# ifftshift of an 8192 x 8192 matrix by DMA alone: half rows in 512 KB DMAs with SBUF copies between them

## The chip, the cores and the metric

The kernel runs on one core of a Trainium2 chip. The metric is the device time in microseconds of one execution, lower is better. A profile of one execution comes with the times.

## The reference

```python
def setup_inputs():
    return {"x": np.random.randn(8192, 8192).astype(np.float32)}

def reference(x):
    return np.fft.ifftshift(x)
```

Both axes have an even length, so the four quadrants change places: output row r, left half, is input row (r + 4096) mod 8192, right half; and the right half comes from the left half of the same input row. Nothing is computed. 268.4 MB are read and as many written.

## The kernel before

The kernel is a set of DMAs from the input in HBM to the output in HBM; nothing passes through SBUF and no compute engine takes part. The unit is a half row: 4096 floats, 16 KB, contiguous in input and output.

One DMA (`copy`, issued on L29) moves 256 half rows, 4 MB. Its pattern is `[[C, 16], [16*C, 16], [1, 4096]]`: the outermost dimension has 16 entries, one for each of the core's 16 DMA engines, and engine e moves rows e, e+16, e+32, ... of the block, 16 half rows in all.

The loop on L36 to L39 goes through the rows in parts of 1024, four DMAs for each queue. SP's queue (`nc.sync`) moves left output halves, in row order. ACT's queue (`nc.scalar`) moves right output halves, and takes the four blocks of a part in the order 2, 3, 0, 1, so that it is 512 rows away from SP.

The two queues are independent of each other: each engine has one ring of descriptors for each of them. The order within a queue is the order of the program. The scheduler gives each queue four completion semaphores, so at most four DMAs of a queue are in flight; the issue of the next waits until the oldest has landed on all 16 engines.

Of the kernel before, what the change touches and what calls it, by code (L numbers as in the profile page):

```python
# [1 line left out]

# [4 lines left out]


ENGINES = 16


@with_exitstack
def kernel(
    ctx: ExitStack,
    tc: tile.TileContext,
    x: bass.AP,
    out: bass.AP,
):
    nc = tc.nc
    R, C = x.shape  # L20
    hr = R // 2
    hc = C // 2
    per = 16
    rows = ENGINES * per

    def copy(queue, row, h, step):

        dims = [[C, ENGINES], [step * C, per], [1, hc]]
        queue.dma_start(  # L29
            out=bass.AP(out.tensor, out.offset + row * C + h, dims),  # L30
            in_=bass.AP(x.tensor, x.offset + (row + hr) % R * C + hc - h, dims),
        )

    for first in range(0, R, 4 * rows):  # L36
        for n in range(4):
            copy(nc.sync, first + n * rows, 0, ENGINES)
            copy(nc.scalar, first + (n + 2) % 4 * rows, hc, ENGINES)  # L39


# [1 line left out]
_INS = ['x']  # L43
_OUTS = [((8192, 8192), 'float32')]


def kernel(**inputs):
    import numpy as _np
    import concourse.bacc as _bacc
    import concourse.tile as _tile  # L50
    from concourse import mybir as _mybir
    from concourse.bass_utils import run_bass_kernel_spmd as _run

    nc = _bacc.Bacc("TRN2", target_bir_lowering=False, num_devices=1)  # L54
    arrays, args = {}, []
    for name in _INS:
        a = _np.ascontiguousarray(inputs[name])
        if a.dtype.kind in "iu":
            a = a.astype(_np.int64)
        arrays[f"in_{name}_dram"] = a  # L60
        args.append(nc.dram_tensor(f"in_{name}_dram", a.shape, _mybir.dt.from_np(a.dtype), kind="ExternalInput").ap())
    for i, (shape, dtype) in enumerate(_OUTS):
        dt = _mybir.dt.from_np(_np.dtype(dtype))
        args.append(nc.dram_tensor(f"out_{i}_dram", shape, dt, kind="ExternalOutput").ap())
    with _tile.TileContext(nc) as tc:
        kernel(tc, *args)
    r = _run(nc, [arrays], core_ids=[0])
    got = tuple(r.results[0][f"out_{i}_dram"] for i in range(len(_OUTS)))
    return got[0]
```

## Time and profile before

| | |
|---|---|
| median of 2 runs | 822.9 us (822.66 and 823.14) |
| span of the profiled execution | 812.4 us |
| time around the span, if the profiled execution took the median | 10.5 us |
| DMAs | 32 on SP's queue, 32 on ACT's, 4 MB each |
| median from issue to landing | 101.0 us on each queue |
| packets | 17,408, 268.44 MB |
| DMA-issuing instruction, median | 571 ns on SP, 578 ns on ACT |

The span runs from the first to the last instruction. "Share of 16 engines" in the DMA part of the page is the time that a queue's packets took, divided by 16 times the span. A packet here is one half row or one semaphore write of 4 bytes. GB/s on the page count each byte once, though it is read from HBM and written to HBM.

### The profile page before, as it was taken

The page shows a single profiled execution, that of the slowest core. Times are in us where ns is not written, and L with a number is a line of the kernel's source. Part 1 is how long each engine was busy: PE and PEld are TensorE (multiplying, and loading weights), DVE is VectorE, ACT ScalarE, POOL GpSimd, SP SyncE. Part 2 cuts the span into 40 slices and gives each one's busy share as a digit, 9 for nine tenths or more (in the row PEclk, how much of TensorE's full clock was granted, in tenths as well). Part 3 has the DMA queues.
Part 4 walks back from the last instruction along what each step waited for, and adds up shares of the span by engine and source line. Part 5 has one row for each costly group of instructions (what it writes and reads, how often), then busy time and mean ns, then how long its engine had stood idle before and what let it go on. Part 6 is the DMA issues. An engine that isn't in the chain of part 4 may idle for free. (4 is left out here: it accounts for less than half of the span.)

```text
span 812.4 us, 109 instructions
## 1 busy us (share of the span) xinstructions
POOL 0.2 (0%) x4
## 2 busy tenths in 40 slices
POOL 0000000000000000000000000000000000000000
DMA  9999999999999999999999999999999999999998
GB/s 307 331 331 336 335 331 331 335 325 337 334 332 336 331 333 332 334 339 332 332 334 331 329 331 334 332 328 333 330 334 335 334 328 333 332 331 330 338 331 280
DMA packets 17408, 268.44 MB, mean 330 GB/s; under 512 B 1024, under 2 KB 1024, under 8 KB 1024
## 3 DMA queue, kind: packets, MB, share of 16 engines
q1 hardware_dynamic: 8704, 134.22, 49.7%
q10 hardware_dynamic: 8704, 134.22, 49.5%
HBM read 268.44 MB, written 268.44 MB: 661 GB/s over the span
## 5 line engine op out<-in xcount | busy, mean ns | idle before, releaser
L54 POOL MEMSET const-bfloat16-1.0<- 128x1 bf16 x1 | 0.1, 101 | 0.0
L54 POOL MEMSET const-uint8-127<- 128x1 uint8 x1 | 0.1, 101 | 0.0
L54 POOL MEMSET const-float32-0.0<- 128x1 f32 x1 | 0.1, 98 | 0.2 <-issue 0.2
L54 POOL MEMSET const-float32-1.0<- 128x1 f32 x1 | 0.1, 98 | 0.0
## 6 DMA issues: line engine op xcount, KB each, us to landing
out_dram<-in_x_dram SPq DMA_DIRECT2D x32, 4096.0 KB, 101.0
out_dram<-in_x_dram ACTq DMA_DIRECT2D x32, 4096.0 KB, 101.0
```

What stands on the lines that cost most here:

```text
L54: nc = _bacc.Bacc("TRN2", target_bir_lowering=False, num_devices=1)
```

## The change

Three things change.

- A DMA moves 32 half rows (512 KB, 2 per engine) instead of 256. The pattern is otherwise the same, and so is the order in which each engine moves its half rows. ACT's queue is still 512 rows from SP's within a part of 1024 rows.
- A tile `idle` of 128 x 2560 floats in SBUF is set to zero by VectorE at the start (L35).
- In the second to the seventh eighth of the rows, each half-row DMA is followed in its queue by a DMA from 16 partitions of `idle` to the same partitions of another SBUF tile (`space`, L49): one piece per engine, of 512, 1024, 1536, 1792, 2048 and 2560 floats, that is 2, 4, 6, 7, 8 and 10 KB. The first and the last eighth have none. The destination tiles come from a pool with six buffers for each of the two queues. What they hold is not used.

The issue order of a step is: SP half rows, ACT half rows, SP copy, ACT copy. Of the four DMAs of a queue in flight, two are then half-row DMAs and two are copies.

```diff
-    per = 16
+    f32 = mybir.dt.float32
+    per = 2
     rows = ENGINES * per
+    longest = 2560
+    still = ctx.enter_context(tc.tile_pool(name="still", bufs=1))
+    spaced = ctx.enter_context(tc.tile_pool(name="spaced", bufs=6))
+    idle = still.tile([128, longest], f32)
+    nc.vector.memset(idle[:], 0.0)
 
-    def copy(queue, row, h, step):
-
-        dims = [[C, ENGINES], [step * C, per], [1, hc]]
+    def copy(queue, row, h):
+        dims = [[C, ENGINES], [ENGINES * C, per], [1, hc]]
+        dst = out.offset + row * C + h
+        src = x.offset + (row + hr) % R * C + hc - h
         queue.dma_start(
-            out=bass.AP(out.tensor, out.offset + row * C + h, dims),
-            in_=bass.AP(x.tensor, x.offset + (row + hr) % R * C + hc - h, dims),
+            out=bass.AP(out.tensor, dst, dims),
+            in_=bass.AP(x.tensor, src, dims),
         )
 
+    def space(queue, n, name):
 
+        into = spaced.tile([128, longest], f32, name=name)
+        queue.dma_start(out=into[0:128:8, :n], in_=idle[0:128:8, :n])
 
-    for first in range(0, R, 4 * rows):
-        for n in range(4):
-            copy(nc.sync, first + n * rows, 0, ENGINES)
-            copy(nc.scalar, first + (n + 2) % 4 * rows, hc, ENGINES)
+    part = 1024
+    for first, n in zip(range(0, R, part), (0, 512, 1024, 1536, 1792, 2048, 2560, 0)):
+        for row in range(first, first + part, rows):
+            other = first + (row - first + part // 2) % part
+            copy(nc.sync, row, 0)
+            copy(nc.scalar, other, hc)
+            if n:
+                space(nc.sync, n, "sync_piece")
+                space(nc.scalar, n, "scalar_piece")
```

## The prediction

> **What bounds the kernel now.** I read the page first (slices, DMA queues, issues), then the waits of the SP queue, then a table of stretches of the span, and last the records of single packets in the trace. No engine computes, so the slices and the queues say it all:
>
> ```profile
> span 812.4 us, 109 instructions
> ...
> DMA  9999999999999999999999999999999999999998
> GB/s 307 331 331 336 335 331 331 335 325 337 334 332 336 331 333 332 334 339 332 332 334 331 329 331 334 332 328 333 330 334 335 334 328 333 332 331 330 338 331 280
> ...
> q1 hardware_dynamic: 8704, 134.22, 49.7%
> q10 hardware_dynamic: 8704, 134.22, 49.5%
> HBM read 268.44 MB, written 268.44 MB: 661 GB/s over the span
> ```
>
> The 16 DMA engines are busy for 99.2% of the span from end to end, half of it for each queue. A half row (4096 floats, 16,384 bytes) is one packet: 16,384 of them, and 1,024 packets of 4 bytes that carry the semaphores (64 DMAs x 16 engines). So one engine moves 1,024 half rows in 0.992 x 812.4 = 806 us, 787 ns each. The packet records give the spread behind that mean: the shortest take 608 to 611 ns, 32% lie within 615 ns, the longest takes 2,064 ns, the standard deviation is 194 ns. So an engine can move a half row in 611 ns (26.8 bytes per ns), and 787 - 611 = 176 ns per half row, 180 us of the 806, is time in which the shared path to memory holds it back. On one engine the half rows of the two queues alternate (96% of neighbours are of different queues), and a 4-byte packet takes 9 ns with no gap before or behind it.
>
> ```profile
> core 0: us, POOL busy (x), PEclk, DMA share, GB/s
> ...
> 3.00:5.00 2.00, 0.00 (x0) 1.00 1.00 393
> 5.00:10.00 5.00, 0.00 (x0) 1.00 1.02 360
> 10.00:20.00 10.00, 0.00 (x0) 1.00 0.99 328
> ```
>
> The stretch from 3 to 5 us has packets of SP's queue alone, 16 engines busy, and shows 393 GB/s; with both queues it falls to 360 and then stays near 330. That is short, and packets are counted where they start, but it says that 330 need not be a wall.
>
> ```profile
> SPq L29 <- DMA out_dram<-in_x_dram: 689.4, 28, 25.3
> ```
>
> Of SP's 32 issues 28 wait: each queue has four DMAs in flight, and the fifth waits for the first to land on its slowest engine.
>
> **The change, part by part.** (1) The main transfers. Row order on every engine, packet size and bytes stay as they are (engine e still moves rows e, e+16, ... of one half, and ACT is still 512 rows from SP). DMAs of 2 instead of 16 half rows per engine make 512 instead of 64. (2) Copies inside SBUF: 64 in each of six eighths, 384 in all, one piece of 2, 4, 6, 7, 8 or 10 KB per engine. They add work to the engines, none to HBM.
>
> *Packets.* Semaphore packets per engine: 512 + 384 = 896 instead of 64, so 832 x 9 ns = 7.5 us more. Copies: 64 x (2+4+6+7+8+10) KB = 2,368 KB per engine. Before shows no copy within SBUF. Its lower price is the engine's fastest rate, 26.8 bytes per ns: 90.5 us. As the upper one I take a copy that is held back as the mean half row is, 16,384/787 = 20.8 bytes per ns: 116.6 us. I take the lower, as a copy does not use the memory path that holds the others back. New engine time: 98 us (124 at the upper price) on 806.
>
> *What of it is given back.* While an engine copies, it does not ask for HBM, and the other 15 queue less. Two bounds: nothing given back, 98 us; all of it given back up to the engine's own floor. For the second, an eighth needs 806/8 = 100.8 us of memory; an engine's own need in the 10 KB eighth is 128 x 0.611 + 64 x 10,240/26.8 ns + 1.2 = 103.8 us, and every other eighth stays below 100.8 (8 KB: 98.9). That bound costs 3 us. In between I use a closed queue: 16 customers (the engines), each 611 ns plus its share of copy away from the crowd, and one shared server of S ns per half row with random service. Waiting for n customers follows from n-1: R = S(1 + Q), X = n/(R + Z), Q = XR, with Z = 611 - S + copy and semaphore time per half row. It gives 787 ns at n = 16 for S = 45.8 ns (358 GB/s each way). The random service is a choice, borne out by the spread: the excess over 611 has a mean of 176 and a deviation of 194 ns, about as an exponential wait has. With the copies in Z, the eighths cost 100.9, 103.7, 106.6, 109.7, 111.4, 113.1, 116.7 and 100.9 us: 863 instead of 806, so +57.5 us. At the upper copy price it is +76 us.
>
> *Issues and the wait.* An issue holds SP 571 ns and ACT 578 (the source line's durations). A pair of main DMA and copy is 1.15 us of issuing per queue, against 2 x 524,288 bytes / 330 GB/s = 3.2 us of moving, so it hides. It would set the pace only if a pair moved in under 1.15 us. The copies stand in the same queues, so four in flight are now two main and two copies. From the last engine's semaphore packet to the next issue of that queue takes 0.8 us (36.68 to 37.48 us in the records), from an issue to its first packet 1.4 us (11.86 to 13.29): 2.2 us. When main DMA i has landed, the slowest engine still has one main DMA and two copies in that queue and as much in the other: four half rows, 3.1 us, plus copies. So the slowest does not run dry; an engine ahead of it by more than 0.9 us may (DMAs land over 1.2 to 2.7 us from first engine to last). A fast engine that pauses is not the one that sets the end, and it eases HBM too; 0 to 10 us, I take 0. The Trainium skill's DMA: Bandwidth & Descriptors, under Rules for kernel authors, wants at least 1 MiB per DMA for the best rate, which speaks against 512 KB; here the packets follow each other over the end of a DMA with no gap, so a row outweighs that rule, and by its fit of 2.0 us plus bytes/436e3 a main DMA alone would be an estimated 3.2 us, just what a queue has for it.
>
> *Hidden at nothing.* The memset of the 128 x 2560 tile lies at the start; the first copy comes after the first eighth, some 100 us later. If it were late, SP and ACT would stop at their first copy with main transfers behind them, and three main DMAs per queue would cover about 10 us. A copy tile is written again after six copies of that name, two more than are in flight. The last eighth has no copies, so the drain of the queues stays as it is.
>
> *Sum.* The profiled execution spans 812.4 us and the median is 822.9, so 10.5 us lie around the span; I leave these alone. 822.9 + 57.5 = 880.
>
> **Rivals.** (A) Hidden: memory moves 661 GB/s whatever the engines do, and the copies fill time in which they would only queue. Then it is +3 to +10 us, 826 to 833. For it: the slices stay within 325 to 339 GB/s. Against: a third of the half rows runs at the engine's own pace, which a path that is always full would not allow. The Trainium skill's HBM Reference, under Specifications (TRN2), gives about 716 GB/s for a domain; the trace's 661 is 92% of it, which leans to this rival.
>
> (B) Nothing given back: the 176 ns are collisions of address patterns, not of numbers of engines. 822.9 + 98 = 921. For it: the mean of a half row changes with its place in the DMA, about 755 to 815 ns by turns. Against: it needs 14 engines in HBM to queue like 16.
>
> (C) Faster, the other side: the spacing takes the two queues out of each other's way, as in the 3 to 5 us stretch. At 393 GB/s a half row takes 16 x 16,384/393 = 667 ns: 1,024 x 0.667 + 98 = 781 against 806, so 798 us. It decides where half rows fall below (806 - 98)/1,024 = 691 ns; over 2% faster needs 675. Against: the fall from 360 to 328 came within 20 us, with both queues in order.
>
> (D) Copies at half rate, because pairs of engines meet in SBUF: 13.4 bytes per ns, 181 us of engine time, by the same queue +126: 949 us. No row of before bears on it. The Trainium skill's SBUF page (SBUF — State Buffer, under Door 1: The DMA port swizzle) has partitions 0, 8, 16, ... on 8 of 16 ports, two engines to each; that would give this rate where both copy at once, and no run here shows it.
>
> **How the numbers follow.** Chances: forecast (840 to 905) 0.43, A 0.20, B 0.13, C 0.17, D 0.07. The range goes from C's 798 to a little over B's 921, 926; it leaves out half of C and most of D, about 0.15. The likeliest case alone, with copy prices of both ends and a third of the give-back either way, is 850 to 905. About 2% is what a measurement of this kernel can tell from no change (806.4 to 839.4): faster 0.17, same 0.20, slower 0.63.
>
> **What would show it.** In the slices the rate should be near 331 GB/s in the first and last eighth and fall step by step between, to about 287 of main bytes in the 10 KB eighth, with the DMA share still 9 throughout. The mean main packet should come down from 787 to about 735 ns, the shortest stay at 611; a 10 KB copy should take about 382 ns. Wrong would be: main packets at 787 (B) or under 691 (C), copies of 760 ns (D), eighths of equal length (A), or DMA shares under 9, where the window of four runs dry.

## The result and the profile after

The changed kernel takes 913.6 us (two runs, 908.0 and 919.3) against 822.9: ratio 1.110, 95% interval 1.094 to 1.126. It is slower, by 91 us. The profiled execution is the one of 919.3 us, with a span of 917.3. So about 2 us lie around a span, not 10.5; the profile of before (812.4 us) was simply one of its quicker executions. The spans of before listed in later runs go from 817.5 to 823.5 us. The changed kernel varies far more: its six executions, these two and the four of the run `again`, take 880.6 to 919.3 us, all at a granted clock of 1.0, so its loss is 58 to 96 us from one execution to the next.

The first view is the page of the changed kernel: span, slices, queues, HBM bytes, and the DMA issues with their size and the median time from issue to landing.

```profile
span 917.3 us, 944 instructions
...
DMA  9999999999999999999999999998999999999998
GB/s 304 324 329 329 334 332 342 350 339 352 347 332 360 339 378 382 320 376 317 307 395 349 302 306 309 337 311 303 351 347 345 330 331 367 313 355 322 327 327 282
...
q10 hardware_dynamic: 18432, 153.65, 50.4%
q1 hardware_dynamic: 18432, 153.65, 46.3%
...
HBM read 268.44 MB, written 268.44 MB: 585 GB/s over the span
...
out_dram<-in_x_dram SPq DMA_DIRECT2D x256, 512.0 KB, 7.9
out_dram<-in_x_dram ACTq DMA_DIRECT2D x256, 512.0 KB, 7.9
```

The slices still show 9 nearly everywhere, but the two queues sum to 96.7% instead of 99.2%, and the rate, steady before, jumps between 302 and 395 from slice to slice (it now counts the copies too). The table of stretches is cut at the start of every 2,048th half row, that is at the eighths of the work:

```profile
core 0: us, DVE busy (x) POOL busy (x), PEclk, DMA share, GB/s
2.20:103.90 101.70, 1.32 (x1) 0.00 (x0) 1.00 1.00 331
103.90:208.90 105.00, 0.00 (x0) 0.00 (x0) 1.00 0.99 339
208.90:318.00 109.10, 0.00 (x0) 0.00 (x0) 1.00 0.96 346
318.00:429.90 111.90, 0.00 (x0) 0.00 (x0) 1.00 0.97 355
429.90:553.20 123.30, 0.00 (x0) 0.00 (x0) 1.00 0.96 332
553.20:680.40 127.20, 0.00 (x0) 0.00 (x0) 1.00 0.94 330
680.40:812.10 131.70, 0.00 (x0) 0.00 (x0) 1.00 0.96 334
812.10:916.10 104.00, 0.00 (x0) 0.00 (x0) 1.00 0.98 324
```

The first and the last eighth, without copies, are as before (101.7 and 104.0 with the drain). The eighths with 2, 4 and 6 KB lie 1.3 to 2.5 us above the values of the prediction's queue; those with 7, 8 and 10 KB jump to 12 to 15 us above. And where the engines have more to do than ever, their share falls to between 0.94 and 0.96: the queues run dry.

The packet records split the 8 KB eighth into what one engine does in its 127.2 us: 128 half rows at their floor of 611 ns, 78.2 us; 64 copies of 317 ns, 20.3; 128 semaphore packets, 1.2; idle (5.7%), 7.3; and 20.2 us by which half rows last longer than their floor (mean 769 ns). That excess looks different from before: 60% of the half rows now are at the floor and some are far above it. Those that follow an idle engine (about 150 in the eighth, which start with no packet ending within 6 ns of them) take about 1,220 ns in the mean; a half row right behind one of the same queue, as the second of a DMA is, takes about 690. A start from idle also costs where there is little other traffic: the first 16 half rows of the kernel before took 940 to 1,306 ns, the next 16 took 611 to 707. A queue that runs dry is paid for twice, in idle time and in a cold start.

### The profile page after: what moved, and what is told of

Its sections match the earlier page's. It is cut to its first block, busy times and chain, and to the rows that moved or that the text cites. A ratio compares the mean times of both kernels' runs of the same rounds, so it can differ in the third digit from the quotient of the medians.

```text
span 917.3 us, 944 instructions
## 1 busy us (share of the span) xinstructions
DVE 2.2 (0%) x1; POOL 0.2 (0%) x4
## 5 line engine op out<-in xcount | busy, mean ns | idle before, releaser
L35 DVE MEMSET idle<- 128x2560 f32 x1 | 2.2, 2192 | 1.3 <-PEq L74 1.3
```

Of the source, the lines that this page charges most:

```text
L35: nc.vector.memset(idle[:], 0.0)
```

## The experiments

Each eighth's length in us, by the length of its copies (the prediction's queue in the first row; `reversed` is sorted by length, so its places differ; the eighths are those of the profiled execution, the time is the median):

| kernel | none, first | 2 KB | 4 KB | 6 KB | 7 KB | 8 KB | 10 KB | time, us |
|---|---|---|---|---|---|---|---|---|
| prediction | 100.9 | 103.7 | 106.6 | 109.7 | 111.4 | 113.1 | 116.7 | 880 |
| changed kernel | 101.7 | 105.0 | 109.1 | 111.9 | 123.3 | 127.2 | 131.7 | 913.6 |
| `reversed` | 102.2 | 105.1 | 109.1 | 117.3 | 122.6 | 132.0 | 128.2 | 913.7 |
| `tiny` (64 B in all six) | 102.2 | 106.3 | 105.0 | 105.6 | 103.6 | 105.1 | 105.7 | 840.2 |
| `per4` | 102.4 | 101.7 | 102.9 | 102.8 | 102.2 | 104.1 | 111.5 | 833.0 |
| `per8` | 101.7 | 103.5 | 102.7 | 103.0 | 102.8 | 103.2 | 104.3 | 837.9 |
| `every4` | 102.0 | 102.4 | 104.6 | 107.8 | 112.6 | 122.9 | 131.9 | 904.3 |

**The small DMAs alone.**

```diff
-    for first, n in zip(range(0, R, part), (0, 512, 1024, 1536, 1792, 2048, 2560, 0)):
+    for first, n in zip(range(0, R, part), (0, 0, 0, 0, 0, 0, 0, 0)):
```

> The 512 KB DMAs alone, no copies in any eighth. Theory W (the window of four DMAs runs dry once two of the four are short copies; the rest is the recursion): without copies four main DMAs, 8 half rows per engine, are in flight, so nothing runs dry and only 448 more semaphore packets of 9 ns per engine are added: 823 to 830 us, eighths of 101 us, DMA share 9 throughout. Rival G (the give-back is missing: copies cost their full time): the same. Rival D512 (the DMA size itself costs): 840 or more, eighths of 103 or more.

Measured: 821.3 us against 822.1 of before, ratio 0.9995 (0.9975 to 1.0015). The fifth eighth and the landing of its DMAs:

```profile
409.30:511.00 101.70, 0.00 (x0) 0.00 (x0) 1.00 1.00 330
...
out_dram<-in_x_dram SPq DMA_DIRECT2D x256, 512.0 KB, 12.8
```

Cutting 4 MB DMAs into 512 KB costs nothing here, as long as four of them are in flight per queue. The rule of at least 1 MiB (the Trainium skill's DMA: Bandwidth & Descriptors, Rules for kernel authors) does not decide in this kernel; the measurement does.

**Does the length or the place set the cost?**

```diff
-(0, 512, 1024, 1536, 1792, 2048, 2560, 0)
+(0, 2560, 2048, 1792, 1536, 1024, 512, 0)
```

> The same kernel with the lengths in reverse order (10, 8, 7, 6, 4, 2 KB in the second to the seventh eighth). If the length of the copies sets the cost of an eighth, the eighths take about 132, 127, 123, 112, 109, 105 us in this order and the total stays at 905 to 920 us. If the place does (addresses of the later eighths, or a drift of the queues that builds up), the sixth and seventh eighth stay above 120 us with copies of 4 and 2 KB, and the second stays below 112.

Measured: 913.7 us, and the eighths follow the length (table), but for those with 8 and 10 KB, which have changed order (132.0 and 128.2 us); that is less than one eighth varies between two executions of one program (8 KB: 127.2 and, in `again`, 114.7). So it is not the addresses, and no drift that builds up. Its four executions go from 883 to 929 us, far wider than before's.

**More half rows behind each place in the window.** The window is what one queue may have in flight, four DMAs. The copies per half row stay the same. Part of the edit (`idle` gets the same middle dimension as `into`, and the pool has three buffers, in `per8` two, instead of six):

```diff
-    per = 2
+    per = 4                      # per8: 8
-    into = spaced.tile([128, longest], f32, name=name)
-    queue.dma_start(out=into[0:128:8, :n], in_=idle[0:128:8, :n])
+    into = spaced.tile([128, 2, longest], f32, name=name)        # per8: 4
+    queue.dma_start(out=into[0:128:8, :, :n], in_=idle[0:128:8, :, :n])
```

> DMAs of 4 half rows per engine (1 MB), each followed by a copy DMA with two pieces per engine: the same copy bytes per half row in each eighth, but twice the half rows behind each of the four DMAs in flight. Theory W: the engines stop running dry, the eighths come down to the recursion's values (103.7, 106.6, 109.7, 111.4, 113.1, 116.7), the sum to 880 to 890 us, and the long half rows that start after an idle engine all but vanish. Rival G (copies bunch on the engines or collide, so their time is not given back): 905 to 920, the eighths of 7, 8 and 10 KB still at 123 to 132 us.

> DMAs of 8 half rows per engine (2 MB), each followed by a copy DMA of four pieces per engine; the same copy bytes again, four times the half rows in flight. Theory W: no better than the 1 MB version by more than 1%, since that one no longer runs dry: 875 to 890 us. Rival G: 905 to 920.

Measured: 833.0 us (ratio 1.014, 1.009 to 1.019) and 837.9 (1.021, 1.019 to 1.023). Theory W was right that this takes the loss away, and wrong about what would be left: not the queue's 880 but almost nothing. Of the 16 us that `per8` keeps, 4 are in its last eighth, which has no copies (108.6 us; 104.3 in `short`). The table of stretches of the 1 MB version:

```profile
core 0: us, DVE busy (x) POOL busy (x), PEclk, DMA share, GB/s
...
309.20:412.00 102.80, 0.00 (x0) 0.00 (x0) 1.00 1.00 386
412.00:514.20 102.20, 0.00 (x0) 0.00 (x0) 1.00 1.01 400
514.20:618.30 104.10, 0.00 (x0) 0.00 (x0) 1.00 1.01 403
618.30:729.80 111.50, 0.00 (x0) 0.00 (x0) 1.00 1.01 394
```

With 6 to 8 KB copies the eighths are as short as without, the DMA share is 1.00 again, and 400 GB/s move, of which some 328 are half rows (2,048 x 16,384 bytes in 102.2 us). The half rows give back what the copies take: in the 7 KB eighth of `per4` their mean is 651 ns instead of 783. In the 10 KB eighth two pieces join into one packet of 20,480 bytes; they take 949 ns in the mean, where the quickest take 761, and there the eighth does grow.

**What fewer engines get from memory.** 12 of the 16 engines move 94% of the half rows; no copies. Part of the edit (the loops and the last blocks, which go to 16 engines, are left out here):

```diff
+    few = 12
+    block = few * per
-        dims = [[C, ENGINES], [step * C, per], [1, hc]]
+        dims = [[C, engines], [engines * C, per], [1, hc]]
```

> The kernel before with 12 of the 16 DMA engines for 15,360 of the 16,384 half rows (outermost dimension of 12), the rest on 16 as before; no copies. It measures what 12 engines get when four ask for nothing. Hard path (memory gives about 330 GB/s to any number of engines that can take it): the half row falls to its floor, 611 to 640 ns, 12 engines move 307 to 322 GB/s, 1,280 x 0.611 to 0.640 + 50 + 17 = 849 to 886 us. Recursion of the prediction: 697 ns, 282 GB/s, 959 us. No give-back (787 ns whatever the number): 1,074 us.

Measured: 837.8 us (ratio 1.018, 1.012 to 1.025), below even the hard path's range; the rest on 16 engines is in it.

```profile
span 835.9 us, 129 instructions
...
DMA  6777777777777777777777777777777777899776
GB/s 279 322 321 325 323 326 323 321 325 324 325 325 321 325 316 323 324 321 325 325 324 324 321 322 326 319 324 322 323 325 325 320 324 323 340 325 328 315 325 274
```

The DMA share is a 7 instead of a 9, and the rate is still about 323 GB/s (most slices show 321 to 325). Half rows take 611 to 616 ns in the mean of each of the first seven eighths, and 97% or more of them are at the floor. So 12 engines hardly queue, and 16 gain only 2% over them. The path is hard: it gives some 330 GB/s each way, and four engines can do something else nearly for nothing. The random service that I chose for the queue is refuted. The Trainium skill's HBM Reference, under Specifications (TRN2), puts a domain at about 716 GB/s; 12 engines drew 642 over the span and 16 drew 661, so both come close to it. The prediction let that figure lean to rival A, in which memory binds and the engines have room, and this run shows that reading to be the right one.

**The places without the copies' time.** Every copy is 64 bytes per engine.

```diff
-(0, 512, 1024, 1536, 1792, 2048, 2560, 0)
+(0, 16, 16, 16, 16, 16, 16, 0)
```

> The changed kernel with every copy cut to 64 bytes per engine in all six eighths: the number of DMAs, the waits and the places in the window stay, the engine time of the copies goes. Theory W (two of the four places in a queue's window are taken by copies, so an engine can run out of half rows and the next one starts cold): the places alone already cost something, 826 to 845 us, eighths two to seven at 102 to 106, some half rows of over 1.2 us behind an idle engine. Rival P (the pauses themselves bunch the engines): 820 to 825 us, eighths of 101.7 as without copies.

Measured: 840.2 us against 823.1 of before, ratio 1.021 (1.015 to 1.027): 17 us, where the small DMAs without copies (`short`) cost nothing. Copies of 11 ns each cost as much as that because each takes a place; on another queue (`pool`, below) far longer ones cost 6 us. Theory W held, P did not. The issues and SP's waits:

```profile
SPq L41 <- DMA out_dram<-in_x_dram: 506.5, 249, 5.2
...
out_dram<-in_x_dram SPq DMA_DIRECT2D x256, 512.0 KB, 6.7
out_dram<-in_x_dram ACTq DMA_DIRECT2D x256, 512.0 KB, 6.8
sync_piece<-idle SPq DMA_DIRECT2D x192, 1.0 KB, 6.1
```

A 1 KB DMA lands 6.1 us after its issue, since it stands in the queue like the rest. Without copies a main DMA lands after 12.8 us (`short`), here after 6.7: the stock in flight has halved, and 2.2 us of it (landing, wake-up, issue, first packet) are always missing.

**The small DMAs, but three or four main ones in flight.** One copy DMA of four pieces after every fourth main DMA. Part of the edit (the tiles get a middle dimension of 4 as in `per8`, and the pool two buffers):

```diff
-            if n:
+            if n and (row - first) // rows % 4 == 3:
```

> 512 KB DMAs as in the changed kernel, but one copy DMA of four pieces per engine after every fourth main DMA instead of one piece after each: the same copy bytes, the same order of packets on an engine as in the 2 MB version, three or four of the four DMAs in flight are main ones. Theory W: 832 to 855 us, most of the loss gone though the DMAs stay at 512 KB. Rival S (small DMAs beside copies cost by themselves, by number of completions): 880 or more.

Measured: 904.3 us (ratio 1.097, 1.090 to 1.104). A miss for W, which gave 832 to 855. The total lies where rival S had it, but the number of DMAs is not the cause either: `short` has as many main ones, the 2 and 4 KB eighths are nearly free, and `pool` below has all of them. The table of stretches and the packet records show another loss:

```profile
core 0: us, DVE busy (x) POOL busy (x), PEclk, DMA share, GB/s
...
531.60:654.50 122.90, 0.00 (x0) 0.00 (x0) 1.00 1.01 341
654.50:786.40 131.90, 0.00 (x0) 0.00 (x0) 1.00 1.01 336
```

The engines are never idle (share 1.01), and these two eighths are about as long as in the changed kernel (127.2 and 131.7). Sampled over the 10 KB eighth, no engine copies for 38% of the time and 12 or more copy at once for 24%; in `per8`, with the same packets in the same order on each engine, 1 to 6 copy for 95% of the time, and never more than 9. My reading is this: in flight are about 8 half rows per queue, one period of the copies; an engine cannot get out of step with the others by more than the window, so all arrive at their copies together. Memory is underused meanwhile (for 33% of the eighth fewer than 8 engines move half rows, in `per8` for 0.3%), and afterwards all 16 queue for it. The copies themselves meet as well: 40,960 bytes take 1,514 ns in most cases of `per8`, but here 3,088 ns in the mean on ACT's queue, 13.3 bytes per ns, half the rate, and 2,490 on SP's. By the Trainium skill's SBUF — State Buffer page (Door 1: The DMA port swizzle) these 16 partitions lie on 8 of 16 ports, from which the prediction's rival D estimated half the rate. The runs agree with it where many engines copy at once, and only there; that the ports are the cause is not shown.

**The copies on a queue of their own.**

```diff
-                space(nc.sync, n, "sync_piece")
-                space(nc.scalar, n, "scalar_piece")
+                space(nc.gpsimd, n, "sync_piece")
+                space(nc.gpsimd, n, "scalar_piece")
```

> The changed kernel with all 384 copies issued on GpSimd's queue instead of behind the half rows: the same DMAs, bytes and sizes, but SP and ACT have four main DMAs in flight again, and an engine takes copies by turns with the two queues rather than at one place in each. If the loss comes from the places that copies take in the queues' windows and from engines copying at the same time (W and bunching): 825 to 850 us. If 384 copies and 512 small DMAs cost by themselves (S): 890 or more.

Measured: 828.2 us, ratio 1.007 (1.005 to 1.009). All 512 small DMAs and all 384 copies are there, and 85 of the 91 us are gone.

```profile
q1 hardware_dynamic: 12288, 134.23, 44.4%
q10 hardware_dynamic: 12288, 134.23, 43.6%
q0 software_dynamic: 12288, 38.82, 11.6%
```

The third queue takes 11.6% of the engines' time, the other two together 88.0 instead of 99.2: the half rows gave nearly all of it back. GpSimd does not wait for the half rows, so the copies do not keep to their eighths here; their number and sizes are the same.

**Bunching without dry queues, a second way, and the yardstick.** `per8` with one buffer per queue for the copies, so that a copy waits for the one before it:

```diff
-    spaced = ctx.enter_context(tc.tile_pool(name="spaced", bufs=2))
+    spaced = ctx.enter_context(tc.tile_pool(name="spaced", bufs=1))
```

> The 2 MB version with one buffer for each queue's copies instead of two, so that a copy waits for the one before it in its queue and fewer DMAs are in flight; at least one main DMA of 8 half rows per engine stays behind, so no engine can run dry. If only dry queues cost (W): within 1% of the 2 MB version, 835 to 845 us. If engines that are held close together copy at the same time and so leave the memory path empty (bunching, as in the run with a copy after every fourth DMA): 845 to 890, with more engines copying at once and copies longer than 26.6 bytes per ns allows, while the DMA share stays at 9.

> The changed kernel once more, on the chip of the two beside it, as their yardstick: 905 to 920 us, eighths as before (105, 109, 112, 123, 127, 132).

Measured: 842.4 us for `per8w` (ratio 1.024, 1.020 to 1.027), 4.5 us over `per8`. The total lies in the range for dry queues alone (835 to 845) and below the one for bunching (845 to 890), so bunching costs little here. One eighth does show it, in one profiled execution: all are as in `per8` except the 10 KB one, 113.0 us instead of 104.3, with copies of 40,960 bytes at about 2,050 ns instead of 1,590 and a DMA share of 9. In that eighth 8 or more engines copy at once for 20% of the time, in `per8` for 1%: a shorter window does bring the copies together, with no queue dry. The changed kernel once more: 912.7 us, its four executions 880.6, 909.5, 915.9 and 916.0. The one of 880.6 was profiled: its eighths are 104.3, 105.0, 112.9, 109.5, 114.7 and 123.2 us, so the loss of one and the same program varies by a third, mostly in the long copies. Engines that fall into step or not would do that; it was not provoked one way or the other, and so it is not shown.

## Why the prediction was right or wrong

The direction was right, and 880 lies 34 us below the measured time. But it got there by two wrong steps that partly cancel: it charged some 50 us too much for what is given back, and some 80 us too little for the window. That the number came out so near is luck.

**The give-back was the wrong model.** The step "a closed queue ... with random service" gave +57.5 us. The excess over the floor does look like an exponential wait, but that is how 16 engines share a path that 12 can fill; it is not what remains when some of them leave. With 12 engines it gives 697 ns per half row, measured were 611 to 616. The bound that I named first, all of it given back (+3 us), is what `per4` (+11 against its own before) and `pool` (+6) nearly reach.

**The window was sized at nothing.** The step "0 to 10 us, I take 0" is the one that failed. I looked at the slowest engine, whose queue does not run dry, and let the others pause for free. The places of the copies alone cost 17 us (`tiny`). With the copies' own time the loss is 91 us, and the engines then copy together more than they need to: in the 10 KB eighth of the changed kernel 8 or more copy at once for 12% of the time, against 1% in `per8` and 36% in `every4`. How those 91 us split between dry queues, cold starts and bunching is not settled: in the 8 KB eighth idle time is 7.3 us and the half rows' excess 20.2 us, and the second holds cold starts (an estimated 5 us: 150 starts, each some 490 ns over the other half rows' 734, on 16 engines) and queueing after a common pause alike. That deeper windows (`per4`, `per8`) or other queues (`pool`) remove nearly all of it is shown.

**Terms that held.** The copies cost what the lower price says: 84, 159, 234, 272, 309 and 385 ns in the median (the estimate for 10 KB was 382, and their mean is 415). Semaphore packets stayed at 9 ns, the shortest half row at 608; issues took 590 to 602 ns in the median instead of 571 to 578, and stayed hidden. The size of the DMAs is free, as the packets' seamless order said. The mean half row of the six eighths came to 758 ns, not the 735 of the signs. And the pattern by place in the DMA, named for rival B, is wider than the 755 to 815 ns given there: by groups of four places on one queue the means of before run from about 740 to 835.

**The rivals.** A (hidden) describes the hardware, and is what `per4` and `pool` show, but the kernel as changed did not allow it. B has the nearest time, 921, with the wrong cause: the addresses do not matter (`reversed`, `eng12`), and the time was not withheld by memory. C did not come about: half rows fell to 723 ns at best in the changed kernel, and where they fell lower (632 in `per4`) the copies took up what they gave. D is refuted as a steady rate (0.6% of the 10 KB copies take over 700 ns) and real where many copies coincide (`every4`). Of the signs named at the end, "DMA shares under 9, where the window of four runs dry" is the one that fired, in the table of stretches rather than in the tenths of the page.

## What to carry to other kernels

A transfer that costs its engine next to nothing still takes a place in its queue's window (11 ns each here, 17 us in all): count the work that remains in flight behind the slowest engine and behind the fastest, against the time from landing to the next first packet. Where a resource is saturated, test how sharp its knee is by taking customers away, before a spread of durations is read as random queueing. And work that is to hide behind a saturated path must be spread over time: the same packets took 837.9 us with 2 MB DMAs in the window (`per8`) and 904.3 with 512 KB ones (`every4`), where the engines turned to their copies together and left the path underused.

## What I had not expected of the hardware

Twelve DMA engines copy HBM to HBM at about 322 GB/s with nearly every half row at 611 ns, and 16 reach only 330; the knee is that sharp. A half row that starts on an engine which had run dry takes about 1,220 ns under this load, the others of that eighth 734 in the mean. And two neighbouring pieces of a copy join into one packet when they are contiguous (20,480 and 40,960 bytes in one record).
